# Block products with a fourth accumulator, down products of a stage's first tiles moved back, norm statistics later in PE's list

## The chip, the core and the metric

The kernel runs on one core of a Trainium2 chip. Its time is device time in microseconds (us) from the start of an execution to its end. Engines are named as in the profile: PE (TensorE: MATMUL, and PEld for its weight loads), DVE (VectorE), ACT (ScalarE), POOL (GpSimd) and SP (SyncE, which here only issues DMAs).

## What is computed

Two transformer-like blocks on 512 tokens of width 1024, all in fp32. Seven stages follow each other on the same residual x:

```python
h  = x + concat(gla(n), mla(n)) @ w_out          # n = rms_norm(x)            stage "mix"
h += square(relu(m @ w_up)) @ w_down             # 1024 -> 4096 -> 1024       stage "mlp"
h += (p @ w_proj) * sigmoid(n @ w_gate + b)      #                            stage "ple"
x += pool_mixer(rmsnorm(x))                      #                            stage "pool"
x += (silu(conv3(n @ w_gate)) * (n @ w_val)) @ w_out   # 1024 -> 2816 -> 1024 stage "ffn0"
x += chunk_attention(rmsnorm(x)) @ w_o           # 16 heads                   stage "att"
x += (silu(conv3(n @ w_gate)) * (n @ w_val)) @ w_out   #                      stage "ffn1"
```

Each stage begins with a norm over the 1024 channels: y = x * rsqrt(mean(x*x) + eps) * gain. The gain is applied to x on the way in; the factor rsqrt(...) of each token is applied to a product after it.

## The kernel before, in words

**Layout.** Activations lie transposed, channels on the 128 partitions and the 512 tokens along the free axis, as eight tiles `x[0..7]` of 128x512. Every operand of a product is split into a high and a low part (ACT rounds to the high part, DVE subtracts), and a product is three matmuls: high*high, high*low, low*high (`mm3`). So each 512 KB block of weights, a *unit*, is loaded into a tile `ws` (seven of them), split into `wh` and `wl` in two halves, and used by 24 matmuls. A splitter task runs two to three units ahead of PE.

**Block products.** The up products of mlp and the gate and value products of ffn0 and ffn1 are done four output tiles at a time (a *quad*). The 1024 input channels form two halves, the tokens two halves, and the four output tiles two pairs, which makes a 2x2 by 2x2 block product; it is done with seven block products and sums of blocks where the plain way has eight. The seven are the rows of `PHASES`: b11, b21, n3, n2, n1, b22, t4, each with the accumulator (PSUM bank) that it adds to, whether it is the first in that bank, and the weight tile that it reads. `quad_step` combines them: after b11 ACT copies bank 0 to `c1`, after b21 DVE adds bank 1 to it; n2, n1 and b22 go on adding in bank 0, and ACT copies the bank after n2 (`u2`) and after n1 (`u4`); n3 starts bank 2. DVE subtracts u4 from bank 2 (`c22`); t4 then adds to bank 2, and DVE subtracts u2 from it. `quad_row` multiplies each finished quarter by the norm's factors, and two quarters make a row that `finish` turns into activations. In the trace all of these banks are `pq`, and `u2`, `u4` are `u`.

**Weights of a quad.** `LOADS` gives the five loads of a quad and their place in the order of loads, counted in units from the quad's first. The tile `sum` is loaded three units early and has a second block added to it by a DMA that adds, on POOL's queue. It is split for n3; then a third block is added (`ADDED`) and it is split for n2; then a fourth, and it is split for b22. The tile `low` also has a block added on POOL's queue.

**First tiles and down units.** A stage's first four output tiles don't go by blocks: `first_tiles` fills four banks `pf` with plain products and waits for nothing but x, while DVE and ACT prepare the blocks of x for the quads (`prep_blocks`, `blocks_low`, `blocks_high`). The norm's statistics (`square`, `stats`) run beside it: squares are added over the eight tiles, PE sums over channels (`pst`), POOL takes the power -0.5, and PE spreads the factors of all tokens over the partitions (`psr`) to the row `R`. `first_out` multiplies the four banks by it. A *down unit* (`pdn`) multiplies finished activations by a block of the down weights into x. Quads are grouped (`QG1`: groups of one; `QG2`: 1, then four groups of 2, then 1 and 1), and down units of a group stand between the products of the next group's quads. `units_quads` writes that order out; `ORDERS` is the order of the seven products in a stage's first quad and in the others, and a tuple says behind which of them down units stand.

**Order of everything.** The program is written by generators that `drive` resumes at build time. `Pace` holds planned free times of each engine and ready times of each tile; a task is resumed when its tiles are planned ready at the time at which PE is planned free, the one with the lowest priority number first. Each engine's list is fixed by that. `sub` and `mul` go to DVE or POOL, whichever is planned to be done first; `help` is a planned extra cost of POOL, and with 1e3 POOL is never taken. It is 0.0 in mix and 1e3 from mlp on.

Of the kernel before, what the change touches and what calls it, by code (L numbers as in the profile page):

```python
# [35 lines left out]
def groups(n, most):  # L36
# [3 lines left out]
    for s in size:  # L40
# [8 lines left out]
QG2 = [1] + [2] * (FF2 // P // 4 - 1) + [1] * 2  # L49

PHASES = (("b11", 0, True, "a11"), ("b21", 1, True, "a12"), ("n3", 2, True, "sum"), ("n2", 0, False, "sum"),
          ("n1", 0, False, "low"), ("b22", 0, False, "sum"), ("t4", 2, False, "a22"))

ORDERS = (0, 1, 2, 3, 4, 6, 5), (2, 0, 1, 3, 4, 6, 5)

LOADS = (("sum", 0, -3, (2,)), ("a11", 0, 1, ()), ("a12", 1, 2, ()), ("low", 2, 1.5, (3,)), ("a22", 3, 5, ()))

ADDED = {2: 3, 3: 1}
GIVEN = {0: "a11", 1: "a12", 4: "low", 5: "sum", 6: "a22"}
# [124 lines left out]
class Block:  # L184
# [5 lines left out]
    PM, PG = 2, 3  # L190
    LAZY = 3, 2
    DEC, SCT = 1, 1
    HELP, TURN = (0.0, 1e3), 1.0

    def __init__(self, ctx, tc, a):
# [86 lines left out]
    def load_units(self, most=None):  # L282
        while (self.n_load < len(self.loads) and self.n_load - len(self.ws_freed) < self.most
               and (most is None or self.n_load < most)):
            _, n, src, cols, name, more = self.loads[self.n_load]
            t = self.sp.tile([P, 1024], F32, tag="ws", bufs=self.NL, name="ws")
            if self.n_load >= self.NL:
                self.pace.ready[t.tensor.name] = self.ws_freed[self.n_load - self.NL]
            self.nc.sync.dma_start(t[:, :cols], src)
            if name is None:  # L290
                self.loaded[n] = t
            else:
                n.tile[name] = t
                for block in more:
                    self.nc.gpsimd.dma_start(t, n.src[block], accum_op=OP.add)
            self.n_load += 1
# [187 lines left out]
    def square(self, norm, x, row=True, late=True):  # L484
        nc = self.nc
        sq = self.slot("sq")
        nc.scalar.activation(sq, x, AF.Square)
        if norm.acc is None:
            norm.acc = sq
        else:  # L490
            (nc.vector if late and norm.count > 5 else nc.gpsimd).tensor_add(norm.acc, norm.acc, sq)
        norm.count += 1
        if norm.count == KD:
            self.spawn(self.stats(norm, row), 1)

    def stats(self, norm, row):
        nc = self.nc
        yield self.room(7)
        yield [norm.acc]
        ps = self.bank("pst")  # L500
        for j in range(NT):
            nc.tensor.matmul(ps[:, j:j + 1], norm.acc[:, j * P:(j + 1) * P], self.ones[:, :1], start=True, stop=True,
                             skip_group_check=True)
        norm.acc = None
        norm.ms = self.small("ms", NT)
        nc.vector.tensor_scalar(norm.ms, ps[:, :NT], 1.0 / DM, EPS, op0=OP.mult, op1=OP.add)
        self.free()
        norm.r = self.power("r", norm.ms, NT)
        if not row:
            return  # L510
        yield [norm.r]
        dg = self.slot("dg")
        for j in range(NT):
            nc.vector.tensor_scalar(dg[:, j * P:(j + 1) * P], self.ident, norm.r[:, j:j + 1], None, op0=OP.mult)
        yield self.room(7)
        yield [dg]
        ps = self.bank("psr")
        nc.tensor.matmul(ps, self.ones, dg, start=True, stop=True)
        R = self.slot("R")
        nc.scalar.activation(R, ps, AF.Copy)  # L520
        self.free()
        norm.R = R
# [714 lines left out]
    @staticmethod  # L1237
    def units_quads(plain, src, downs, sizes):

        quads, units, order, wait = [Quad(src[4 * i:4 * i + 4]) for i in range(sum(sizes) - 1)], [], [], []  # L1240
        q, left = -1, sum(sizes)
        for g, n in enumerate(sizes):
            for i in range(n):
                left -= 1
                if q < 0:
                    order.append((q, 0))
                    units += plain
                else:
                    most = -(-len(wait) // (n - i)) if left else len(wait) - 2
                    for at, ph in enumerate(ORDERS[q > 0]):  # L1250
                        order.append((q, ph))
                        units.append(("quad", quads[q], ph))
                        for _ in range((4, 3, 6, 1)[:min(most, len(wait))].count(at)):
                            order.append(wait[0][:2])
                            units.append(wait.pop(0)[2])
                q += 1
            for w in wait:
                order.append(w[:2])
                units.append(w[2])
            wait = [("down", (g, u), x) for u, x in enumerate(downs[g])]  # L1260
        for w in wait:
            order.append(w[:2])
            units.append(w[2])
        return units, order
# [28 lines left out]
    def quads(self, norm, order, sizes, last, after, take, finish, late=None):  # L1293


        group = []
        for g, n in enumerate(sizes):
            group += [g] * n
        acts = [[None] * (n * last) for n in sizes]
        self.finish = finish  # L1300
        ps = quad = None
        for what, i in order:
            if what == "down":
                g, u = i
                yield from self.down(acts[g], u, after if g == len(sizes) - 1 else lambda m: None)
                continue
            if what < 0:
                yield from self.first_tiles(norm, take, acts[0])
                continue
            block, acc, first, _ = PHASES[i]  # L1310
            if quad is None:
                if late is not None and what == sum(sizes) - 2:
                    self.spawn(late(), 5)
                ps, quad = [None] * 3, {"norm": norm, "take": take, "rows": [None, None], "left": [2, 2],
                                        "acts": acts[group[what + 1]], "at": what + 1 - group.index(group[what + 1])}
            yield from self.unit(8, P)
            unit = self.got
            if first:
                yield self.room()
                ps[acc] = self.bank("pq%d" % acc)  # L1320
                self.pace.again.add(ps[acc].tensor.name)
            else:
                name = (None, None, None, "c1", "u2", "u4", "c22")[i]
                yield lambda: name in quad
                yield [quad[name]]
            b = norm.blocks[block]
            for k in range(4):
                yield lambda: b[k] is not None
                for w in range(2):
                    yield [*unit, *b[k]]  # L1330
                    self.mm3(ps[acc][:, w * 256:(w + 1) * 256], (unit[0][:, 4 * w + k], unit[1][:, 4 * w + k]), b[k],
                             first and k == 0 and w == 0, k == 3)
            self.used(ps[acc])
            if i != 2:
                self.spawn(self.quad_step(i, ps, quad), -3)
            if i == 5:
                ps = quad = None

    def quad_step(self, i, ps, quad):

        s, v = self.nc.scalar, self.nc.vector
        yield [ps[PHASES[i][1]]]
        if i in (0, 3, 4):
            name = {0: "c1", 3: "u2", 4: "u4"}[i]
            t = self.slot(name)
            s.activation(t, ps[0], AF.Copy)
            quad[name] = t
        if i == 1:
            yield lambda: "c1" in quad
            t = quad["c1"]  # L1350
            yield [t]
            v.tensor_add(t, ps[1], t)
            self.free()
            self.spawn(self.quad_row(quad, 0, 0, t), -2)
        elif i == 4:
            yield [t, ps[2]]
            v.tensor_sub(t, ps[2], t)
            quad["c22"] = t
            self.spawn(self.quad_row(quad, 1, 1, t), -2)
        elif i == 5:  # L1360
            yield from self.quad_row(quad, 0, 1, ps[0])
            self.free()
        elif i == 6:
            t = quad["u2"]
            yield [t, ps[2]]
            v.tensor_sub(t, ps[2], t)
            self.free()
            self.spawn(self.quad_row(quad, 1, 0, t), -2)

# [394 lines left out]
    def main(self, stages):  # L1764
# [13 lines left out]
        for i, st in enumerate(stages):  # L1778
# [8 lines left out]
            else:  # L1787
                nxt = None
                after = self.store
            yield from run[st](norm, after)  # L1790
            self.lazy, self.help, self.most = self.LAZY[1], self.HELP[1], self.NL
            norm = nxt


# [163 lines left out]
```

## Time and profile before

| | |
|---|---|
| time, median of 3 runs | 1721.99 us (1721.39 to 1725.96) |
| the profiled execution: time, span | 1723.74 us, 1722.0 us |
| mean granted clock of PE | 0.981 |
| busy: PE, DVE, ACT, POOL | 1645.4, 1256.3, 882.0, 265.5 us |
| DMA | 224.85 MB, 131 GB/s |

The span runs from the first instruction to the last. A busy PE has a matmul in it; its matmuls overlap. The granted clock is given as a share of 2.4 GHz, and in this trace it is 1.0 or 0.5. Stages by the trace: mix to 277 us, mlp to 628, ple and pool to 709, ffn0 to about 1084, att to about 1345, then ffn1.

### The profile page before, as it was taken

Reading aid. Unit: us, or ns where it says so; the run is one execution under the profiler, and the core shown is the slowest. Engines: PE = TensorE matmul, PEld = TensorE weight load, DVE = VectorE, ACT = ScalarE, POOL = GpSimd, SP = SyncE. Lnnn points to the kernel's source line nnn. Section 1 sums busy time; section 2 is a strip of 40 time slices with the busy share of each in tenths; the row PEclk is TensorE's granted clock in tenths of the full one; section 3 lists DMA queues with packets and bytes.
Section 4 is the critical chain, followed back from the end, with each engine's and each line's share of the span. In section 5 each row is a group of like instructions: output and inputs, shape, how many; then the busy total and the mean of one; then the engine's idle time right before and its main releaser. Section 6 shows DMA issues by size and latency. Waiting matters only on the chain. (4 is left out here: it accounts for less than half of the span.)

```text
span 1722.0 us, 27741 instructions
## 1 busy us (share of the span) xinstructions
PE 1645.4 (96%) x10640; PEld 1469.7 (85%) x10640; DVE 1256.3 (73%) x2436; ACT 882.0 (51%) x1711; POOL 265.5 (15%) x296
## 2 busy tenths in 40 slices
PE   7989899899999999989999998999999999999998
PEld 6878777799999978879999987989897789999896
DVE  7976769566666757978777767576679878777776
ACT  6635455444444545835454444466656655554542
POOL 3432212001000011211111100221210211111100
PEclk9999999899999999989999999999999999999999
DMA  7101222566666424267677654322223257776751
GB/s 271 50 26 37 85 76 80 133 167 160 161 162 165 150 86 126 62 153 194 177 194 198 174 147 123 111 74 75 74 86 86 86 141 203 186 202 175 180 139 49
DMA packets 66390, 224.85 MB, mean 131 GB/s; under 512 B 7617, under 2 KB 9554, under 8 KB 66258
## 3 DMA queue, kind: packets, MB, share of 16 engines
q1 hardware_dynamic: 50706, 166.46, 27.8%
q0 software_dynamic: 15552, 56.63, 18.9%
q8 instruction: 83, 1.36, 0.3%
q14 instruction: 49, 0.40, 0.1%
HBM read 220.96 MB, written 2.10 MB: 130 GB/s over the span
## 5 line engine op out<-in xcount | busy, mean ns | idle before, releaser
L147 ACT ACTIVATE wh<-ws 128x512 fp32r<-128x512 f32 x690 | 392.7, 621 | 289.7 <-PE pdn L147 140.6
L147 DVE TENSOR_TENSOR wl<-ws,wh 128x512 fp32r<-128x512 f32 x682 | 451.1, 703 | 87.3 <-ACT wh L147 87.0
L147 PE MATMUL pq<-xsh,wh 128*128 128x256 f32 x864 | 246.8, 286 | 4.3 <-ACT u L147 4.3
L147 PE MATMUL pq<-xsl,wh 128*128 128x256 f32 x864 | 245.2, 284 | 0.0
L147 PE MATMUL pq<-xsh,wl 128*128 128x256 f32 x864 | 245.1, 284 | 0.0
L147 DVE TENSOR_TENSOR x<-x,pdn 128x512 f32<-128x512 f32 x177 | 119.8, 682 | 122.6 <-PE pdn L147 122.6
L147 PEld LDWEIGHTS pq<-xsh,wh 128*128 128x128 f32 x864 | 166.3, 192 | 7.4 <-ACT u L147 5.5
L147 PEld LDWEIGHTS pq<-xsl,wh 128*128 128x128 f32 x864 | 166.4, 193 | 1.9 <-issue 0.7
L147 POOL DMA_DIRECT2D ws<-in_w_f x80 | 70.4, 895 | 631.7 <-DVE wl L147 381.1
L147 PEld LDWEIGHTS pq<-xsh,wl 128*128 128x128 f32 x864 | 166.4, 193 | 0.0
L147 PE MATMUL pdn<-yh,wh 128*128 128x512 f32 x352 | 140.2, 398 | 6.4 <-ACT yh L147 6.4
L147 PE MATMUL pdn<-yl,wh 128*128 128x512 f32 x352 | 140.0, 398 | 3.5 <-DVE yl L147 3.4
L147 PE MATMUL pdn<-yh,wl 128*128 128x512 f32 x352 | 138.4, 393 | 0.0
L147 PE MATMUL pq<-xch,wh 128*128 128x256 f32 x432 | 123.1, 285 | 1.9 <-ACT wh L147 1.9
L147 PE MATMUL pq<-xch,wl 128*128 128x256 f32 x432 | 123.3, 286 | 1.2 <-DVE wl L147 1.2
L147 PE MATMUL pq<-xcl,wh 128*128 128x256 f32 x432 | 122.9, 284 | 0.0
L147 PE MATMUL paq<-wh,xsh 128*128 128x256 f32 x384 | 111.4, 290 | 1.8 <-DVE akk L147 1.8
L147 PE MATMUL paq<-wh,xsl 128*128 128x256 f32 x384 | 108.6, 283 | 0.0
L147 PE MATMUL paq<-wl,xsh 128*128 128x256 f32 x384 | 108.6, 283 | 0.0
L147 PE MATMUL pdn<-hh,wh 128*128 128x512 f32 x256 | 101.3, 396 | 4.7 <-ACT hh L147 4.7
L147 PE MATMUL pdn<-hl,wh 128*128 128x512 f32 x256 | 101.5, 397 | 0.9 <-DVE hl L147 0.8
L147 PE MATMUL pdn<-hh,wl 128*128 128x512 f32 x256 | 100.6, 393 | 0.0
(329 smaller groups left out, 3902.7 us busy)
## 6 DMA issues: line engine op xcount, KB each, us to landing
ws<-in_w_f SPq DMA_DIRECT2D x108, 512.0 KB, 4.0
ws<-in_w_f POOLq DMA_DIRECT2D x80, 512.0 KB, 5.5
ws<-in_w_fo SPq DMA_DIRECT2D x44, 512.0 KB, 4.2
ws<-in_w_up SPq DMA_DIRECT2D x39, 512.0 KB, 3.4
ws<-in_w_down SPq DMA_DIRECT2D x32, 512.0 KB, 3.3
ws<-in_w_up POOLq DMA_DIRECT2D x28, 512.0 KB, 5.5
ws<-in_w_out SPq DMA_DIRECT2D x8, 512.0 KB, 3.4
ws<-in_w_gate SPq DMA_DIRECT2D x8, 512.0 KB, 3.2
```

The source lines that it names most:

```text
L147: return call(*args, **kw)
```

## The change

- t4 gets a bank of its own (accumulator 3, the first in it), and stands ahead of n1. After n2 DVE subtracts u2 from bank 2 at once (a new instruction in each quad), after n1 it subtracts u4 from bank 2, which is then free, and after t4 it adds bank 3. PE no longer waits for c22.
- The loads of `low` and `a22` change places in the order of loads.
- Down units stand behind other products: none in the first quad after the first tiles, and later in the others.
- `stats` gets priority -4 instead of 1, and for all norms but the first the sum of squares and the tile for `psr` are planned ready 2.0 us later.
- `help` is set by stage: 1e3 in mlp, ffn0 and ffn1, and 0.0 in mix, ple, pool and att.
- The planned ready time of a load's tile is that of the load `most` places earlier (three in mix, seven later) instead of seven.

```diff
 PHASES = (("b11", 0, True, "a11"), ("b21", 1, True, "a12"), ("n3", 2, True, "sum"), ("n2", 0, False, "sum"),
-          ("n1", 0, False, "low"), ("b22", 0, False, "sum"), ("t4", 2, False, "a22"))
-ORDERS = (0, 1, 2, 3, 4, 6, 5), (2, 0, 1, 3, 4, 6, 5)
-LOADS = (("sum", 0, -3, (2,)), ("a11", 0, 1, ()), ("a12", 1, 2, ()), ("low", 2, 1.5, (3,)), ("a22", 3, 5, ()))
+          ("n1", 0, False, "low"), ("b22", 0, False, "sum"), ("t4", 3, True, "a22"))
+ORDERS = (0, 1, 2, 3, 6, 4, 5), (2, 0, 1, 3, 6, 4, 5)
+LOADS = (("sum", 0, -3, (2,)), ("a11", 0, 1, ()), ("a12", 1, 2, ()), ("low", 2, 2.5, (3,)), ("a22", 3, 4, ()))
...
+    LATE = 2.0
...
-            if self.n_load >= self.NL:
-                self.pace.ready[t.tensor.name] = self.ws_freed[self.n_load - self.NL]
+            if self.n_load >= self.most:
+                self.pace.ready[t.tensor.name] = self.ws_freed[self.n_load - self.most]
...
-            self.spawn(self.stats(norm, row), 1)
+            self.spawn(self.stats(norm, row), -4)
...
     def stats(self, norm, row):
         nc = self.nc
+        late = 0.0 if norm.gain == self.GAIN["mix"] else self.LATE
+        self.pace.ready[norm.acc.tensor.name] += late
...
+        self.pace.ready[dg.tensor.name] += late
         yield self.room(7)
         yield [dg]
...
-                    most = -(-len(wait) // (n - i)) if left else len(wait) - 2
+                    most = 0 if q == 0 else -(-len(wait) // (n - i)) if left else len(wait) - 2
...
-                        for _ in range((4, 3, 6, 1)[:min(most, len(wait))].count(at)):
+                        for _ in range(((5, 2, 6, 3) if i else (5, 6, 4, 3))[:min(most, len(wait))].count(at)):
...
-                ps, quad = [None] * 3, {"norm": norm, ...
+                ps, quad = [None] * 4, {"norm": norm, ...
...
-                name = (None, None, None, "c1", "u2", "u4", "c22")[i]
+                name = (None, None, None, "c1", "u2", "u4")[i]
                 yield lambda: name in quad
-                yield [quad[name]]
...
-        if i == 1:
+        if i == 3:
+            yield [t, ps[2]]
+            v.tensor_sub(t, ps[2], t)
+        elif i == 1:
...
         elif i == 4:
             yield [t, ps[2]]
             v.tensor_sub(t, ps[2], t)
-            quad["c22"] = t
+            self.free()
...
         elif i == 6:
             t = quad["u2"]
-            yield [t, ps[2]]
-            v.tensor_sub(t, ps[2], t)
+            yield [t, ps[3]]
+            v.tensor_add(t, ps[3], t)
...
+            self.help = self.HELP[st in self.QUADS]
             yield from run[st](norm, after)
-            self.lazy, self.help, self.most = self.LAZY[1], self.HELP[1], self.NL
+            self.lazy, self.most = self.LAZY[1], self.NL
```

## Rows read from the trace of the kernel before

**Rows 1.** The page's first part: busy us (share of the span) xinstructions

```profile
PE 1645.4 (96%) x10640; PEld 1469.7 (85%) x10640; DVE 1256.3 (73%) x2436; ACT 882.0 (51%) x1711; POOL 265.5 (15%) x296
```

**Rows 2.** Busy by windows: stretch, its length, busy of each engine, PEclk, DMA share, GB/s

```profile
861.00:904.05 43.05, 43.05 (x318) 41.13 (x317) 34.20 (x59) 22.91 (x41) 5.25 (x6) 1.00 0.75 194
...
284.00:324.00 40.00, 32.82 (x151) 25.59 (x150) 29.58 (x61) 20.57 (x42) 6.77 (x6) 0.87 0.48 111
726.00:770.00 44.00, 35.74 (x194) 29.81 (x193) 33.26 (x64) 19.13 (x35) 7.96 (x7) 0.88 0.56 144
1362.00:1400.00 38.00, 32.77 (x177) 28.13 (x175) 29.24 (x58) 18.84 (x37) 6.54 (x5) 0.87 0.55 139
```

**Rows 3.** Waits of PE: who waited for whom, us in total, times, longest

```profile
PE pst L147 <- DVE sq L147: 7.8, 5, 2.4
```

**Rows 4.** Timeline of PE, ffn1's last quad: start, us, instruction, [idle before, releaser]

```profile
1681.61 0.38 PE L147 MATMUL pq<-xsh,wh 128*128 128x256 f32 x1 [0.69 <-ACT u L147]
...
1687.88 0.80 PE L147 MATMUL pq<-xt,wh 128*128 128x256 f32 x2 [3.13 <-DVE u L147]
...
1692.10 0.28 PE L147 MATMUL pq<-xsh,wh 128*128 128x256 f32 x1
```

**Rows 5.** Timeline of PE, the first group of one quad, ffn0 and ffn1

```profile
993.01 0.40 PE L147 MATMUL pdn<-yh,wh 128*128 128x512 f32 x1
...
1003.10 0.28 PE L147 MATMUL pq<-xsh,wh 128*128 128x256 f32 x1
...
1629.62 0.40 PE L147 MATMUL pdn<-yh,wh 128*128 128x512 f32 x1
...
1638.47 0.28 PE L147 MATMUL pq<-xsh,wh 128*128 128x256 f32 x1
```

**Rows 6.** Timeline of PE, mlp's first quad: down unit, two products, down unit

```profile
308.32 0.49 PE L147 MATMUL pdn<-hh,wh 128*128 128x512 f32 x1
...
323.66 0.28 PE L147 MATMUL pq<-xch,wh 128*128 128x256 f32 x1
...
329.41 0.40 PE L147 MATMUL pdn<-hh,wh 128*128 128x512 f32 x1
...
334.88 0.28 PE L147 MATMUL pq<-xsh,wh 128*128 128x256 f32 x1
```

**Rows 7.** Timeline of PE, first quads: ffn0 n1 and t4; ffn1 n2, n1, t4

```profile
753.80 0.38 PE L147 MATMUL pq<-xsh,wh 128*128 128x256 f32 x1 [0.75 <-ACT u L147]
...
768.46 0.40 PE L147 MATMUL pq<-xt,wh 128*128 128x256 f32 x2
...
1388.43 0.39 PE L147 MATMUL pq<-xch,wh 128*128 128x256 f32 x1 [0.56 <-ACT wh L147]
...
1395.25 0.38 PE L147 MATMUL pq<-xsh,wh 128*128 128x256 f32 x1 [0.75 <-ACT u L147]
...
1405.00 0.40 PE L147 MATMUL pq<-xt,wh 128*128 128x256 f32 x2
```

**Rows 8.** Timeline of POOL and ACT, ffn0's first quad

```profile
739.32 1.84 POOL L147 DMA_DIRECT2D ws<-in_w_f  x2 [3.35 <-DVE xsl L147]
...
748.52 3.76 ACT L147 ACTIVATE wh<-ws 128x512 fp32r<-128x512 f32 x7 [0.78 <-DMA ws<-in_w_f]
```

**Rows 9.** Timeline of POOL and DVE, pool stage

```profile
714.67 1.29 POOL L147 TENSOR_TENSOR sq<-sq 128x512 f32<-128x512 f32 x1 [0.45 <-ACT sq L147]
...
713.61 2.90 DVE L147 TENSOR_TENSOR wl<-ws,wh 128x512 fp32r<-128x512 f32 x2
```

**Rows 10.** Groups of DVE over the span: busy us, mean ns of one | idle before

```profile
L147 DVE TENSOR_TENSOR wl<-ws,wh 128x512 fp32r<-128x512 f32 x682 | 451.1, 703 | 87.3 <-ACT wh L147 87.0 <-issue 0.2
...
L147 DVE TENSOR_TENSOR u<-pq,u 128x512 f32<-128x512 f32 x54 | 37.3, 691 | 60.7 <-ACT u L147 33.8 <-PE pq L147 26.9
```

**Rows 11.** Tile wl: on POOL (ns min/median/max, first and last start); on DVE in att

```profile
L147 POOL TENSOR_TENSOR wl<-ws,wh x8: 1265/1289/1358, 34.4 to 243.4; 128x512 fp32r<-128x512 f32 x8
...
1075.00:1345.00 270.00, 41.83 (x65) 1.00 0.26 84
```

More of the change, by code (lines that the diff above doesn't have):

```diff
@@ L1313, in quads @@
                     self.spawn(late(), 5)
-                ps, quad = [None] * 3, {"norm": norm, "take": take, "rows": [None, None], "left": [2, 2],
+                ps, quad = [None] * 4, {"norm": norm, "take": take, "rows": [None, None], "left": [2, 2],
                                         "acts": acts[group[what + 1]], "at": what + 1 - group.index(group[what + 1])}
```

## The prediction

> **What bounds the kernel now.** I read the page's first part, then the busy time by windows, the PE waits, and the PE timeline at each place where the windows show a gap. The page has PE busy 1645.4 us of a span of 1722.0 [rows 1]: no other engine comes near, so only two things can be won, the 76.6 us in which PE idles and the time at half clock. The windows say where they are not: in the middle of a stage PE is busy 43.05 of 43.05 us at clock 1.00 with DVE at 34.2 [rows 2]. They are at the beginnings of the three stages of block products. In 284 to 324 (mlp) PE idles 7.2 us and the mean clock is 0.87; in 726 to 770 (ffn0) 8.3 us and 0.88; in 1362 to 1400 (ffn1) 5.2 us and 0.87 [rows 2]. I price the clock as window times its deficit (0.5 is 1.2 GHz, 1.0 is 2.4): 5.2, 5.3 and 4.9 us, so 12.4, 13.5 and 10.2 us lie over each beginning. Idle and price of the clock overlap a little; I leave that to the range.
>
> **Unit prices.** A block product lasts 2.87 us (n3 and n2 fill 323.66 to 329.41) and a down unit 5.47 (329.41 to 334.88) where nothing waits [rows 6].
>
> **Step 1: fourth accumulator, t4 ahead of n1.** Today t4 accumulates onto n3's bank, so PE must wait until n1 is done, ScalarE has copied it and VectorE has subtracted it. In the middle of a stage down units lie between, and hide it. The last quad of ffn1 has none: n1 begins at 1681.61 after a wait of 0.69 for the copy, t4 at 1687.88 after 3.13, b22 at 1692.10 [rows 4]. That is 6.27 + 4.22 us for two products worth 5.74, so 4.75 lost (the wait, and t4 at half clock). After the change n2, t4, n1 and b22 follow each other; the wait of 0.7 moves from ahead of n1 to ahead of b22, the rest has no cause left. ffn0's last quad has the same order; I count it alike: 9.5 us for both. mlp's last quad keeps two down units and gives nothing.
> What it adds: a third subtraction a quad, 27 in all at 0.69 us [rows 10], 18.7 us of DVE. In mid stage DVE has 8.9 us free in 43 [rows 2] and a quad with its downs is shorter than that window, so the cover is ample: 0 there. At a beginning it costs what is counted in step 3. It also adds a PSUM bank: three are held by a quad instead of two while down units ask for room, and t4 of a stage's first quad must wait until the first tiles leave one of their four; with three products ahead of it (8.6 us) I cost that at 0, bounds 0 and 3 a stage.
>
> **Step 2: later places for down units.** Where ffn's groups go from two quads to one, the first down unit stands behind only two products and reads activations of the quad just ended: 993.01 to 1003.10 and 1629.62 to 1638.47 [rows 5], 10.09 and 8.85 us for 5.47, so 8.0 lost. In the new order four products stand ahead of it, 5.7 us more, which is over the 4.6 and 3.4 it was late. 8.0 won. In the other quads the downs only move behind work that is there anyway: 0.
>
> **Step 3: the three beginnings.** The first quad loses its down units to the end of its group (mlp) or to the next quad (ffn). mlp's first lasts from 308.32 to 323.66, 9.9 us too long [rows 6]. In ffn0, n1 and the down unit take 753.80 to 768.46, 14.66 for 8.34; in ffn1 1395.25 to 1405.00, 9.75 [rows 7]: 6.3 and 1.4 lost. The statistics add their share: PE waited 7.8 us in five places for the sum of squares, 2.4 at most [rows 3]; the 2 us of LATE cover nearly all.
> What is late next is n2. Its tile is n3's tile with one more block added by a DMA on POOL's queue, issued only when n3's split has been read. In ffn0 POOL issues it at 739.32, and ScalarE's split, waiting for that DMA, begins at 748.52 [rows 8]: 9.2 us. If PE reaches n2 sooner, it waits there. In ffn1 the same product lasts 6.82 us, 1388.43 to 1395.25 [rows 7]. In mlp the two down units that hid this DMA are gone. The loads of low (later) and a22 (sooner) move with it on SP's queue and, for low's own addition, on POOL's, so that less stands ahead of n2's addition; a gain of 0 to 3 us in each stage, of which I take 1.
> The second limit is DVE. It was busy 29.6, 33.3 and 29.2 us in these windows [rows 2] and does not get less (0.7 more each). So at most 9.7, 10.0 and 8.1 us can go there, 27.8 together; the low end is 0, or 3 us lost if n2's wait brings the half clock with it. The downs of mlp are the surest, so I take 8, 6.5 and 5: 19.5 us. The new wait of n1's copy ahead of b22 costs 0.7 in each first quad: 2.1.
> Two of the five waits for the statistics lie in ple and the attention stage, outside the windows; at the mean of 1.6 [rows 3] they are 3.1, of which I take 2.5. The inverse root and the row of factors come up to 4 us later; in ple eight products, in the others the first quad lie between, so 0, bounds 0 and 2 a norm.
>
> **Step 4: POOL helps again.** The last lines of the diff are not in its title: with `help` at 0.0 in ple, pool and att the planner may give a split's subtraction to POOL when DVE is behind. POOL did 8 in mix at 1.29 us [rows 11]; DVE takes 0.70 [rows 10], and att alone has 65 of them [rows 11]. The two engines disturb each other: with POOL's addition running from 714.67, DVE's pair of 713.61 took 2.90 us instead of 1.41 [rows 9, 10]; it lost 1.5, and I put that at 0.8 for each of its two. So a move saves DVE 0.7, costs it up to 0.8 and delivers 0.6 later. Bounds: 5 us won (seven moves where DVE is short and nothing is held up) to 91 lost (all of att's 65 at 1.4). At mix's 8 I expect about eight in att and six in ple and pool, 14 in all, most of them under PE's work; I take 3 lost.
> The Trainium skill, page "SBUF — State Buffer", section "Who interferes with whom", says that a VectorE instruction with two SBUF inputs contends with a GpSimd instruction that reads SBUF, and that the one behind is fully blocked. By that, 14 moves cost DVE 14 x (1.29 - 0.70) = 8 us, an estimate with the durations of this trace; by the row it is 14 x (0.8 - 0.7), about 1. The trace agrees in kind, with 0.8 of 1.3.
>
> **The sum.** 9.5 + 8.0 + 19.5 + 2.5 + 3 x 1 for the loads = 42.5 won; 2.1 + 3 lost; another 4.5 taken off because the whole list of work is planned anew, and the stretches that have no wait now can get one (bounds 2 won, 10 lost). 33 us won. The profiled execution took 1723.74 (span 1722.0 and 1.74 around it), 1.75 over the median of the runs. 1723.74 - 33 = **1691 us**.
>
> **Rivals.**
> - *n2 and DVE keep the beginnings* (0.26). The products get to n2 sooner and wait there for the addition. For it: the 9.2 us of [rows 8], and DVE busy to three quarters in windows that are full of PE waits. Against it: the 9.9 us of mlp's down unit were a wait for activations, not for weights. Then 9.5 + 8.0 + 2.5 stay, and of the beginnings a net 1 after the other losses: 21, **1703 us**.
> - *Nothing moves* (0.08). On top of the first rival the fourth bank delays t4 by its 3 us in each of three beginnings (9), and the late row of factors costs its 2 in five norms (10). 21 - 19 = 2 us: **1722 us**. For it: eight banks, four of them under first tiles. Against it: the row's factors are needed only after three products.
> - *POOL's help slows it* (0.08). One mechanism, in att, ple and pool: POOL's subtraction holds up DVE's, and splits come late to a PE that is nearly full. For it: the pair of [rows 9]. Against it: only 8 operations went to POOL in all of mix [rows 11]. It decides when the loss passes the rest of the gain, 36 us: some 26 moves at 0.6 + 0.8 with no cover. With 32 moves it is 45 lost against 36: **1733 us**. The page of the Trainium skill named under step 4 describes that hold.
> - The forecast, 1680 to 1700, has 0.58.
>
> **Range and chances.** 1676 to 1712: the low end has the beginnings at their DVE limit (8 more) and no loss from planning or POOL (7.5 more), the high end takes in the first rival with 8 us lost to POOL. The last two rivals stay out, 0.16, with 0.04 below. 0.3% is 5.2 us, about what measurements of this kernel can tell apart. Faster: 0.58 + 0.26 = 0.84; same 0.08; slower 0.08.
>
> **What will show it.** The PE wait "pq <- DVE u" goes, and t4 in the last quads lasts 2.9 us; the group u<-pq,u counts 81. Down units last 5.5 us at both switches. PE's pst waits fall below 2 us in all. In the beginnings: a wait of n2 ("pq <- ACT wh") of 1 to 4 us each if I am right, 5 or more with half clock if the first rival is. DVE's busy time is near 1275. POOL's count of wl, 8 now, says how much step 4 did; above 35, with new idle PE time between 1075 and 1345, I am wrong on it. A total of PE idle and half clock not reduced by a third would show the whole forecast wrong.

## The result, and the profile after

The changed kernel takes **1682.09 us**, median of 4 runs (1680.26 to 1685.6), against 1723.97 (1721.39 to 1726.4) of the kernel before in the same comparison: ratio 0.976, 95% interval 0.9734 to 0.9785. 41.9 us are won; 33 were predicted (1691), in a range of 1676 to 1712. The number lies in the range, but the sum behind it was right in two terms only. Other terms were some 9 us too high, and gains of some 20 us were not in it; that these partly cancel is luck.

The profiled execution took 1680.26 us (span 1678.5, mean clock 0.992). First part of its page, beside [rows 1]:

```profile
PE 1626.3 (97%) x10640; PEld 1459.2 (87%) x10640; DVE 1262.8 (75%) x2444; ACT 882.0 (53%) x1714; POOL 282.4 (17%) x312
```

PE idles 52.2 us where it idled 76.6, 24.4 less. The other 19 us are clock: 1722 us at a deficit of 0.019 is 32.7, 1678.5 at 0.008 is 13.4. So both reserves that the prediction named were drawn on.

The same windows as in [rows 2], moved along so that they lie at the same distance from the stage's first tile (length, busy of PE, PEld, DVE, ACT, POOL, PEclk, DMA share, GB/s; the first is in the middle of ffn0):

```profile
841.96:885.01 43.05, 43.05 (x301) 40.41 (x301) 35.89 (x63) 23.77 (x42) 4.34 (x5) 1.00 0.71 194
271.69:311.69 40.00, 36.23 (x230) 32.13 (x229) 33.96 (x68) 25.74 (x51) 5.02 (x6) 1.00 0.56 145
706.96:750.96 44.00, 37.28 (x239) 34.35 (x239) 33.84 (x68) 20.61 (x38) 5.55 (x6) 0.88 0.59 154
1325.55:1363.55 38.00, 31.19 (x197) 28.01 (x195) 28.48 (x57) 18.64 (x36) 5.13 (x7) 0.96 0.50 131
```

Only mlp's beginning is mended (3.8 us of idle at full clock, where idle and clock had cost 12.4). ffn0's still loses 6.7 idle and 5.3 of clock, ffn1's 6.8 and 1.5. A window of fixed length holds more of the stage's work than before (239 matmuls for 194 in ffn0's), so these figures say where time is still lost, not what was won.

PE's waits (us in total, times, longest), beside [rows 3]:

```profile
PE pq L147 <- ACT u L147: 10.1, 8, 2.1
PE pl L147 <- ACT wh L147: 7.8, 1, 7.8
PE pq L147 <- ACT wh L147: 5.3, 3, 3.3
PE pdn L147 <- DVE yl L147: 3.0, 4, 1.8
PE psr L147 <- DVE dg L147: 2.2, 1, 2.2
```

The waits for the squares (7.8 us) and for DVE's u (t4 in the last quads, [rows 4]) are gone. Largest are now waits for the copy u by ACT: 10.1 us in eight, where before they were 4.3 us in six. (The wait of pl is at the start of the kernel, 8.6 us before.) DVE's groups, beside [rows 10], and POOL's share of the splits, beside [rows 11]:

```profile
L147 DVE TENSOR_TENSOR wl<-ws,wh 128x512 fp32r<-128x512 f32 x665 | 437.0, 699 | 91.0 <-ACT wh L147 90.8
...
L147 DVE TENSOR_TENSOR u<-pq,u 128x512 f32<-128x512 f32 x81 | 55.6, 688 | 45.3 <-ACT u L147 35.2 <-PE pq L147 10.1
```

```profile
L147 POOL TENSOR_TENSOR wl<-ws,wh 128x512 fp32r<-128x512 f32 x25 | 33.3, 1347 | 114.0 <-ACT wh L147 85.0 <-issue 28.9
```

81 subtractions of u, as counted. Of the 25 splits on POOL, by the counts of a_help (4) and a_helpatt (21) below, 4 lie in mix, 17 in att and 4 in ple and pool: 21 by the help, where 14 were expected. DVE's busy time is 1262.8 us where 1275 was forecast, since those splits left it. Idle time and price of the clock fell from 109.3 to 65.6 us, by more than the third that the prediction had named as its sign.

**By stage**, from PE's timeline (a stage of block products begins with its first `pf` matmul, ple with `ppj`, att with `paq`; ffn1 is counted to PE's last matmul, 4.0 us ahead of the span's end). By this, att ends at 1349.7 us in the kernel before. The kernels of the experiments below stand in the same table:

| us | mix | mlp | ple, pool | ffn0 | att | ffn1 |
|---|---|---|---|---|---|---|
| before | 276.95 | 351.23 | 80.72 | 374.94 | 265.86 | 368.27 |
| **after** | 264.69 | 344.26 | 80.91 | 364.83 | 258.56 | 361.22 |
| b_load | 264.30 | 353.11 | 80.70 | 375.16 | 265.78 | 368.21 |
| b_help | 274.61 | 352.42 | 84.33 | 376.00 | 260.29 | 373.56 |
| b_statslate | 274.65 | 349.00 | 79.49 | 380.63 | 264.02 | 373.23 |
| a_only_quads | 273.88 | 348.89 | 77.82 | 371.13 | 265.08 | 366.77 |
| a_help | 264.31 | 344.21 | 80.42 | 364.78 | 264.04 | 361.53 |
| a_helpatt | 267.80 | 346.42 | 80.42 | 364.42 | 258.58 | 361.68 |
| a_olddowns | 265.77 | 354.52 | 81.16 | 381.65 | 258.58 | 378.33 |
| a_t4first | 264.16 | 347.37 | 80.78 | 368.09 | 258.60 | 369.14 |
| a_lowlate | 266.60 | 346.05 | 80.90 | 368.44 | 258.57 | 363.88 |
| a_lowlate_t4 | 266.93 | 347.26 | 80.63 | 366.26 | 258.55 | 361.34 |
| a_low15 | 264.69 | 349.59 | 85.50 | 361.39 | 258.58 | 361.03 |
| a_pool0 | 264.99 | 344.37 | 79.50 | 364.92 | 258.58 | 360.99 |

One row is one execution. Between executions with the same list of PE, mix varied by up to 3.6 us, mlp by up to 2.2 and att by less than 1. The three stages that the prediction spoke of gave 24.1 us of the 43.5. **mix gave 12.3 and att 7.3**, where it had expected nothing and a loss.

### The profile page after: what moved, and what is told of

It is laid out like the page before. It is cut to its first block, busy times and chain, and to the rows that moved or that the text cites. A ratio compares the mean times of both kernels' runs of the same rounds, so it can differ in the third digit from the quotient of the medians.

```text
span 1678.5 us, 27783 instructions
## 1 busy us (share of the span) xinstructions
PE 1626.3 (97%) x10640; PEld 1459.2 (87%) x10640; DVE 1262.8 (75%) x2444; ACT 882.0 (53%) x1714; POOL 282.4 (17%) x312
## 3 DMA queue, kind: packets, MB, share of 16 engines
q1 hardware_dynamic: 50706, 166.46, 28.1%
## 5 line engine op out<-in xcount | busy, mean ns | idle before, releaser
L147 DVE TENSOR_TENSOR wl<-ws,wh 128x512 fp32r<-128x512 f32 x665 | 437.0, 699 | 91.0 <-ACT wh L147 90.8
L147 PE MATMUL pq<-xsh,wh 128*128 128x256 f32 x864 | 246.6, 285 | 10.1 <-ACT u L147 10.1
L147 PEld LDWEIGHTS pq<-xsh,wh 128*128 128x128 f32 x864 | 167.1, 193 | 12.9 <-ACT u L147 11.7
```

Of the source, the lines that this page charges most:

```text
L147: return call(*args, **kw)
```

## Experiments

The first four each put one part of the change into the kernel before.

**b_load**: the planner's due times of loads alone.

```diff
-            if self.n_load >= self.NL:
-                self.pace.ready[t.tensor.name] = self.ws_freed[self.n_load - self.NL]
+            if self.n_load >= self.most:
+                self.pace.ready[t.tensor.name] = self.ws_freed[self.n_load - self.most]
```

> The kernel before with one edit of the change alone: the planner's due time of a load goes by the number of loads in flight (3 in the mix stage, 7 later), not by the 7 buffers. Theory: the profiles show mix 12.3 us shorter after the change, and this edit is the only one that orders PE's list anew in mix, so the whole of it comes here: 1711 to 1713 us, all of the difference ahead of the first tile of mlp. Rival: mix is shorter because the statistics of the norms stand elsewhere or because POOL helps, and the order of the loads is worth nothing: 1722 to 1726 us.

Measured: 1715.92 us, ratio 0.994 (0.9918 to 0.9962): 8 to 10 us. mix is 12.65 shorter than in the profile of before, about 10 shorter than in the three others that leave mix alone. mlp is 1.9 longer, but its list of PE is that of before, so this is no effect of the edit. Theory held as to the place; the time lies between its 1711 to 1713 and the rival's 1722. Two stretches of mix in the kernel before, then in this one (columns as above), and PE's waits of mix in each:

```profile
80.00:100.00 20.00, 16.17 (x105) 13.52 (x103) 16.04 (x46) 10.18 (x22) 9.42 (x19) 0.83 0.10 40
180.00:200.00 20.00, 16.27 (x107) 13.39 (x106) 15.22 (x49) 5.79 (x14) 3.27 (x4) 0.83 0.00 0
```

```profile
80.00:100.00 20.00, 19.27 (x146) 16.46 (x144) 18.39 (x56) 8.93 (x23) 6.93 (x10) 1.00 0.08 27
180.00:200.00 20.00, 18.23 (x144) 15.06 (x145) 17.10 (x56) 6.97 (x16) 6.54 (x11) 1.00 0.32 103
```

```profile
PE mt L147 <- DVE prob L147: 6.1, 6, 2.0
PE po L147 <- DVE sct L147: 5.6, 4, 1.9
```

```profile
PE mt L147 <- DVE prob L147: 1.9, 2, 1.6
...
PE po L147 <- DVE sct L147: 1.0, 1, 1.0
```

Before, PE stood idle 3.8 us in each stretch and the clock fell. The two groups of waits, 11.7 us, shrink to 2.9. With due times that fit the three loads in flight, the planner puts other matmuls (x146 for x105 in the first stretch) into these gaps.

**b_help**: POOL's help in ple, pool and att alone.

```diff
+            self.help = self.HELP[st in self.QUADS]
             yield from run[st](norm, after)
-            self.lazy, self.help, self.most = self.LAZY[1], self.HELP[1], self.NL
+            self.lazy, self.most = self.LAZY[1], self.NL
```

> The kernel before with one edit alone: POOL may take a weight split's subtraction in ple, pool and the attention stage. Theory: the attention stage's 7.3 us come from here, ple and pool get nothing: 1716 to 1718 us, POOL's count of such subtractions 8 + 14 to 18. Rival one (my prediction): the help costs about 3 us: 1725 to 1728. Rival two: attention is shorter because its statistics come later: 1722 to 1726 here, with its stage as long as before, 266 us.

Measured: 1729.64 us, ratio 1.0027 (1.0011 to 1.0043), by the ratio slower by 4.6 us (2 to 7). Theory and my prediction were each half right: att is 5.6 shorter, but ple and pool 3.6 longer and ffn1 5.3. The trace shows where: in the pool stage PE has one new wait, 2.9 us for ACT's xsh, and in ffn1's first quad it waits 2.4 us for wh, 2.3 for yh and 1.0 for yl, where before it waited 0.6, 0.5 and 0.2. What made these late is not shown.

**b_statslate**: statistics later alone (priority -4, and 2 us on `norm.acc` and `dg`).

```diff
-            self.spawn(self.stats(norm, row), 1)
+            self.spawn(self.stats(norm, row), -4)
...
+        self.pace.ready[norm.acc.tensor.name] += late
...
+        self.pace.ready[dg.tensor.name] += late
```

> The kernel before with one edit alone: the statistics of a norm 2 us later in PE's list. Prediction: PE's waits for the sum of squares fall from 7.8 us to under 2 us; 2.5 us of them in ple and attention, the rest at the beginnings of the block product stages: 1717 to 1720 us. Rival: PE only waits for the next thing instead (weights, activations), since the work of VectorE and ScalarE ahead of it is the same: 1722 to 1725 us with the same idle time of PE.

Measured: 1726.79 us, ratio 1.0008 (0.9993 to 1.0023): nothing won. The prediction fell; the rival's 1722 to 1725 was near. ple, pool and att are 3.1 shorter, mlp 2.2, but ffn0 5.7 and ffn1 5.0 longer. In ffn0 the row of factors (psr) comes 32.7 us behind the stage's first tile, 28.1 before. PE reaches the first quad's down unit 0.8 us sooner, and its activations come 3.2 later; this kernel:

```profile
756.65 0.80 PE L147 MATMUL pdn<-yh,wh 128*128 128x512 f32 x1 [6.24 <-ACT yh L147]
757.38 0.80 PE L147 MATMUL pdn<-yl,wh 128*128 128x512 f32 x1
```

6.24 us of wait, and then matmuls of 0.8 us where 0.4 is normal, at a granted clock of 0.50 (756.65 to 762.00).

**a_only_quads**: the edits of `PHASES`, `ORDERS`, `LOADS`, `units_quads`, `quads` and `quad_step` alone.

```diff
+ORDERS = (0, 1, 2, 3, 6, 4, 5), (2, 0, 1, 3, 6, 4, 5)
...
+                    most = 0 if q == 0 else -(-len(wait) // (n - i)) if left else len(wait) - 2
```

> The kernel before with the edits of the block products alone: the fourth accumulator, the new order of the seven products, the moved loads and the later places of the down products; statistics, loads' due times and POOL's help as before. Theory (the parts add up by stages): mlp, ffn0 and ffn1 give 24 us together less what the later statistics give, mix, ple, pool and attention nothing: 1700 to 1705 us. Rival one: the later statistics are needed for it, and without them the beginnings keep their stalls: 1708 to 1712. Rival two: the parts do not add up, replanning decides: under 1695 or over 1715.

Measured: 1707.53 us, ratio 0.9898 (0.9874 to 0.9922). 17.6 us, but only 7.6 in the three stages (2.3, 3.8, 1.5), not 24: the parts don't add up by stages, and the total lies just short of rival one's numbers. What is left, in the first quad of ffn0:

```profile
734.45 2.05 PE L147 MATMUL psr<-dg,ones 128*128 128x512 f32 x2 [4.34 <-DVE dg L147]
```

PE waits 4.3 us for the row of factors. The row itself is late: DVE had what the inverse root needs at 727.5, but in POOL's list low's own addition stands ahead of the root and waits 15.5 us for low's load:

```profile
731.46 0.88 POOL L147 DMA_DIRECT2D ws<-in_w_f  x1 [15.53 <-DMA ws<-in_w_f]
732.07 1.33 POOL L147 TENSOR_TENSOR r<-ms,mhalf 128x4 f32<-128x4 f32 x1
```

That wait is not what the total lacks, though. In ffn0 and ffn1 the first quad ends as soon as in a_help below, which has the later statistics (56.7 us behind the stage's first tile for 57.4, and 55.1 for 54.6). The difference, 6.4 and 5.2 us, lies in the first down unit of the third quad: 11.91 and 12.24 us here, 6.05 in both stages there. In ffn0 it stands between these two rows, and its longest wait is 1.75 us, for yl:

```profile
806.58 0.40 PE L147 MATMUL pdn<-yh,wh 128*128 128x512 f32 x1
...
818.50 0.28 PE L147 MATMUL pq<-xsh,wh 128*128 128x256 f32 x1
```

So the two parts need each other: the later statistics win nothing on the kernel before, and some 15 us on this one (a_help). Why the operands of that down unit come late without them is open. The four ratios multiplied give 0.987; the change has 0.976.

The next kernels take one part out of the changed kernel or alter it.

**a_help**: POOL's help undone (the diff of b_help, reversed).

> The changed kernel with POOL's help in ple, pool and attention undone. So far the help alone, on the kernel before, cost 4.6 us: attention 5.6 shorter, ple and pool 3.6 longer, ffn1 5.3 longer. Theory one (it costs the same within the change): attention 5.6 longer, ple and pool 3 shorter, ffn1 4 to 5 shorter than after the change: 1677 to 1681 us. Theory two (the later order at ffn1's beginning takes its loss away and keeps its gain): attention 5 to 7 longer, ffn1 the same, ple and pool 3 shorter: 1684 to 1687 us.

Measured: 1686.58 us, ratio 0.9768 (0.9741 to 0.9795). Theory two, but for ple and pool, which it had 3 us shorter: att is 5.5 longer, all other stages are within 0.5 us, ffn1 too. Within the change the help wins 5.5 us in att and costs nothing that shows. The totals, with intervals that overlap, don't show it by themselves; the stage does, which took 258.55 to 258.60 us in all eight kernels that have the change's list there. PE's waits in att, here and in the changed kernel:

```profile
PE ao L147 <- ACT probT L147: 4.8, 5, 1.4
PE paq L147 <- DVE akk L147: 1.8, 3, 0.6
```

```profile
PE at L147 <- DVE prob L147: 2.0, 3, 1.4
PE paq L147 <- DVE akk L147: 1.2, 2, 0.6
```

The five waits for probT go when POOL takes splits. Set beside a_only_quads, which differs from a_help by the late statistics and by mix's due times (which alone moved none of these stages beyond what executions differ, b_load), the late statistics give mlp 4.7, ffn0 6.4, ffn1 5.2 and att 1.0, and cost ple and pool 2.6.

**a_helpatt**: the help in mix and att only.

```diff
-            self.help = self.HELP[st in self.QUADS]
+            self.help = self.HELP[st not in ("mix", "att")]
```

> The changed kernel with POOL's help in the attention stage alone, not in ple and pool. Theory: ple and pool lose their 3 us (81 to 78, as in the kernel with the block products' edits alone), ffn0 does not change, attention keeps its 258.6: 1678 to 1680 us. Rival: the 3 us are not POOL's, but come from the later statistics: 1681 to 1684.

Measured: 1684.34 us, ratio 0.9747 (0.9719 to 0.9775). ple and pool stay at 80.4: rival held as to the stage: the 3 us there are not POOL's.

**a_olddowns**: the old places of the down units in the new order.

```diff
-                    most = 0 if q == 0 else -(-len(wait) // (n - i)) if left else len(wait) - 2
+                    most = -(-len(wait) // (n - i)) if left else len(wait) - 2
...
-                        for _ in range(((5, 2, 6, 3) if i else (5, 6, 4, 3))[:min(most, len(wait))].count(at)):
+                        for _ in range((4, 3, 6, 1)[:min(most, len(wait))].count(at)):
```

> The changed kernel with the old places of the down units: in the first quads, and in the switches from two quads to one behind two products. Prediction: the two switches lose 8 us again (first down unit there 10.1 and 8.9 us instead of 5.5), and the three first quads get their down units back, with waits for the activations, 12 to 20 us: 1702 to 1710 us. Rival: with the fourth accumulator the first quads' time is set by DVE and ScalarE, with the downs in it or not, and only the switches lose: 1688 to 1692 us.

Measured: 1728.1 us, ratio 1.0007 (0.999 to 1.0024). 46 us worse than the change, more than either forecast: without the new places the change gives nothing in all. mix and att keep their 18 us, and mlp, ffn0 and ffn1 lose 20 against the kernel before. PE's waits, and ffn0's first down unit, of this kernel:

```profile
PE pdn L147 <- ACT yh L147: 22.8, 8, 9.8
PE pq L147 <- ACT u L147: 18.5, 27, 0.7
```

```profile
751.83 0.80 PE L147 MATMUL pdn<-yh,wh 128*128 128x512 f32 x1 [9.79 <-ACT yh L147]
```

The first line is the expected part: first quads and switches. The second is one I had not thought of: in the new order b22 stands behind n1 in every quad, and must wait 0.7 us for its copy unless a down unit lies between, in all 27 quads. The place "5" in the new tuple is that cover. In my working the wait was counted in the three first quads alone.

**a_t4first**: t4 ahead of n2 in first quads, a22 loaded one place earlier.

```diff
-ORDERS = (0, 1, 2, 3, 6, 4, 5), (2, 0, 1, 3, 6, 4, 5)
+ORDERS = (0, 1, 2, 6, 3, 4, 5), (2, 0, 1, 3, 6, 4, 5)
...
```

> The changed kernel with t4 ahead of n2 in the first quad of mlp, ffn0 and ffn1, and a22's load one place earlier. Theory: n2 waits 0.5, 1.4 and 3.3 us for the weights that the addition on POOL's queue completes, and runs at half clock after it; with t4's 2.9 us ahead the wait goes in mlp and ffn0 and falls under 1 us in ffn1. Against it n1 then stands right behind n2 and waits 0.7 to 1 us for its copy: 3 to 6 us won in all, 1676 to 1679 us. Rival: DVE and ScalarE prepare the blocks and weights of the whole first quad late, so each product that comes sooner waits by as much (t4's activations are the last that are prepared): 1681 to 1684 us, with the same end of the first quad.

Measured: 1695.07 us, ratio 0.9821 (0.9794 to 0.9848), 13 us worse than the change; both fell. n2's wait did fall (3.5 to 2.6 us in ffn1, none in the others), but n1 waits 4.6 to 6.1 us for the copy of n2. ACT's timeline in ffn1 of this kernel shows why:

```profile
1356.75 2.19 ACT L147 ACTIVATE wh<-ws 128x512 fp32r<-128x512 f32 x4 [5.04 <-DMA ws<-in_w_f]
...
1364.72 2.19 ACT L147 ACTIVATE wh<-ws 128x512 fp32r<-128x512 f32 x4 [5.07 <-DMA ws<-in_w_f]
1366.82 0.57 ACT L147 ACTIVATE u<-pq 128x512 f32<-128x512 f32 x1
```

The copy u stands behind a split of weights that waits 5 us for the addition by DMA. ACT takes its list in order, so a late DMA holds a copy that has all it needs. The changed kernel has the same in small; in ffn1 n1 waits 1.10 us for this copy:

```profile
1356.68 1.15 ACT L147 ACTIVATE wh<-ws 128x512 fp32r<-128x512 f32 x2 [4.16 <-DMA ws<-in_w_f]
1357.74 0.58 ACT L147 ACTIVATE u<-pq 128x512 f32<-128x512 f32 x1
```

**a_lowlate**: low's own addition issued at the split of n2's weights.

```diff
...
+        if ph in (3, 4) and "low" in quad.tile and not quad.summed:
+            nc.gpsimd.dma_start(quad.tile["low"], quad.src[3], accum_op=OP.add)
+            quad.summed = True
```

> The changed kernel with one thing moved: low's own addition on POOL's queue is issued at the split of n2's weights, not at low's load. In the changed kernel it stands first in POOL's queue at each of the three beginnings and waits 15 to 16 us there for low's load; the inverse root of the norm (POOL) and n2's addition stand behind it. Theory (POOL's queue holds the beginnings): the root comes 6 us sooner, PE's wait for dg (2.2 us in ffn0) goes, n2's waits of 1.1, 1.7 and 3.5 us go or fall under 1, and the half clock after them with it: 1670 to 1677 us. Rival (the beginnings are bound by DVE's and ScalarE's work, the queue only looks late): n2 waits less and n1 or b22 by as much more, 1680 to 1684 us. Rival two: low's addition now lands too late for n1, slower than after the change: 1685 to 1692.

Measured: 1689.15 us, ratio 0.979 (0.977 to 0.9811), 7 us more than the change by the medians, though the intervals overlap. ffn0 and ffn1 are 3.6 and 2.7 longer. That is in the second rival's range, but not by its mechanism (n1 waits for no weights). The theory's first step was there: n2's waits fall from 1.67 and 3.51 to 0.98 and 1.00 in ffn0 and ffn1, and the second quad begins 7 us sooner in both. But then PE stands before the first down unit, 6.70 and 6.53 us; ffn1 in this kernel:

```profile
1383.66 0.80 PE L147 MATMUL pdn<-yh,wh 128*128 128x512 f32 x1 [6.53 <-ACT yh L147]
1384.39 0.80 PE L147 MATMUL pdn<-yl,wh 128*128 128x512 f32 x1
```

The operand yh was held by ACT's list, as the copy u was in a_t4first. DVE's last step ahead of it (qr) ends at 1377.12, but a split that waits for an addition stands before it:

```profile
1376.43 0.69 DVE L147 TENSOR_TENSOR qr<-qr,fb 128x512 f32<-128x512 f32 x1
```

```profile
1379.67 2.19 ACT L147 ACTIVATE wh<-ws 128x512 fp32r<-128x512 f32 x4 [4.26 <-DMA ws<-in_w_f]
...
1382.99 0.61 ACT L147 ACTIVATE yh<-qr 128x512 fp32r<-128x512 f32 x1
```

ffn0 has the same, with a wait of 4.44 us. In the changed kernel this yh is done 55.4 us behind the stage's first tile, and PE comes to its unit at 63.5. So the first tiles' activations were not late by themselves: in a_lowlate the input of yh was there when PE came (1377.13). The moved addition brings n2 forward and makes a later split late. One wait of 6.53 us, and a unit behind it that lasts 10.4 us for 5.47 (granted clock 0.50 to 1391 us), cost more than the 7 us won before it.

**a_lowlate_t4**: both of the last two.

> The same with t4 ahead of n2 in the first quads as well. In the changed kernel that order cost 13 us, since n1 then waited 4.6 to 6.1 us for the copy of n2's product, which stood in ScalarE's queue behind splits that waited for additions. Theory: with POOL's queue free those splits are no longer late, and n2 has 2.9 us more time: the wait for the copy falls to about 0.7 to 1 us, 1668 to 1675 us. Rival: the split of b22's weights waits for the addition that follows n2's split whatever stands before, and the copy stays behind it: 1683 to 1690 us, slower than the kernel with the moved addition alone.

Measured: 1686.98 us, ratio 0.9776 (0.9755 to 0.9798): in the rival's range, but not slower than a_lowlate, as it had said. Its mechanism is there: n1 waits 3.3 to 5.5 us for the copy of n2 in all three first quads. The two edits together don't help either.

**a_low15**: low and a22 loaded at the old places.

```diff
-... ("low", 2, 2.5, (3,)), ("a22", 3, 4, ()))
+... ("low", 2, 1.5, (3,)), ("a22", 3, 5, ()))
```

> The changed kernel with the loads of low and a22 back at their old places (low one place earlier, a22 one later). Prediction: the moved loads are worth 0 to 3 us a stage, about 1: 1683 to 1686 us here. Rival (low's addition stands ahead of n2's on POOL's queue with either place, and an earlier load lets it pass sooner): n2's waits at the beginnings fall: 1676 to 1680 us.

Measured: 1685.1 us, ratio 0.9766 (0.9745 to 0.9786): 3.0 us by the medians, as predicted, though the two intervals overlap. It is not 1 us a stage: mlp loses 5.3 (ACT's split ahead of the copy waits 4.60 for its DMA there, and n1 4.96 for the copy), ple and pool 4.6 (PE waits 2.8 us for ACT's xsh there, as in b_help), and ffn0 wins 3.4.

**a_pool0**: no late statistics in the pool stage, the one place where they cost. The list of PE differs in this alone.

```diff
-        late = 0.0 if norm.gain == self.GAIN["mix"] else self.LATE
+        late = 0.0 if norm.gain in (self.GAIN["mix"], self.GAIN["pool"]) else self.LATE
```

> The changed kernel with the 2 us of delay for the statistics taken away in the pool stage alone; in PE's list the sum of squares there moves 24 matmuls (2.9 us) forward, and nothing else does. In the changed kernel it stands after the last pu product, with nothing behind it that PE could do while POOL and VectorE finish the factors: it takes 2.84 us to the next matmul instead of 0.8 to 0.9, and pp then waits 1.90 us for u. Theory: both go, ple and pool fall from 80.9 to 78 us, the rest is as after the change: 1678 to 1680.5 us, 2 to 3 under the changed kernel. Rival: the sum of squares is not ready 2.9 us sooner (VectorE's last additions), PE waits ahead of it instead and the stage stays at 80 to 81 us: 1681 to 1684 us.

Measured: 1680.45 us, ratio 0.975 (0.9726 to 0.9774). ple and pool 79.5 instead of 80.9, half of what was expected; both sides were half right. PE there, changed kernel, then this one:

```profile
677.43 0.95 PE L147 MATMUL pst<-ones,sq 128*128 128x1 f32 x8
680.27 2.07 PE L147 MATMUL pp<-pm,u 128*128 128x144 f32 x8 [1.90 <-DVE u L147]
```

```profile
675.92 1.05 PE L147 MATMUL pst<-ones,sq 128*128 128x1 f32 x8 [1.51 <-DVE sq L147]
...
681.28 1.97 PE L147 MATMUL pp<-pm,u 128*128 128x144 f32 x15
```

pp no longer waits, but the sum of squares now does, 1.51 us. The kernel has the lowest median of all, but its interval overlaps the change's: no gain over it is shown.

## Why the prediction came out as it did

The terms, with "lost" as the length of PE's blocks over 2.88 us a product, 5.47 a down unit and 5.44 a first tile's unit, summed over the place:

| term | predicted | lost before -> after | won |
|---|---|---|---|
| two last quads | 9.5 | 5.8 -> 0.9, 5.6 -> 0.9 | 9.5 |
| two switches | 8.0 | 4.6 -> 0, 3.4 -> 0 | 8.0 |
| three beginnings, new waits and loads in them | 19.5 - 2.1 + 3 | 13.7 -> 6.7, 18.8 -> 14.6, 14.7 -> 12.8 | 13.1 |
| statistics in ple, pool, att | 2.5 | att 1.8; ple and pool gained about nothing | 2 |
| POOL's help | -3 | att 264.04 -> 258.56 (a_help, after) | 5.5 |
| replanning, the rest of the three stages | -4.5 | ends 3.4 -> 6.4, middles 3.4 more | -6 |
| mix's due times | not in the sum | b_load | 10 to 12 |

**Right.** Step 1 and step 2, to a tenth of a microsecond in all: t4 in the last quads takes 2.88 us, with the wait of 0.7 moved to b22 as forecast, and the down units at the switches take 5.47. ffn1 after the change, last quad (t4, n1, b22) and switch:

```profile
1641.13 0.40 PE L147 MATMUL pq<-xt,wh 128*128 128x256 f32 x2
...
1644.01 0.28 PE L147 MATMUL pq<-xsh,wh 128*128 128x256 f32 x1
...
1647.73 0.38 PE L147 MATMUL pq<-xsh,wh 128*128 128x256 f32 x1 [0.69 <-ACT u L147]
```

```profile
1599.13 0.40 PE L147 MATMUL pdn<-yh,wh 128*128 128x512 f32 x1
...
1604.59 0.40 PE L147 MATMUL pq<-xt,wh 128*128 128x256 f32 x2
```

Both were read as a wait at one place with its cover counted out. The n2 waits of 1.1, 1.7 and 3.5 us lie in the 1 to 4 that I had named.

**Too large: step 3.** The sentence that fell short is "What is late next is n2". Late next were also the copies by ACT: six waits of 0.7 to 2.1 us, 8.7 together, for the 2.1 that I took. n1's stand behind splits that wait 1.7 to 4.2 us for a DMA, and b22's 2.1 us in ffn0 and ffn1 behind the work that piled up on ACT after such a split. Where n2 came sooner (a_t4first, a_lowlate), the same list held the copy, or the first activation. The bound by DVE, 27.8, was no near one: ACT waiting in order for DMAs came first. mlp, where four covered down units follow, won 7.0 of the net 8.3 that I gave it, ffn0 4.2 of 6.8, ffn1 1.9 of 5.3.

**Wrong in sign: step 4.** I priced a moved split by what it does to DVE (0.7 saved, up to 0.8 lost) and took the cover for granted. In att the chain runs over ACT's probT, and 17 moved splits took five waits of it away. On the kernel before, the same edit does cost 4.6 us, by its effect on the stages beside att; the trace shows the waits there, not what makes them. The pair in [rows 9] was misread a little: the first of its two subtractions lost 0.46 us to an earlier addition on POOL, the second 1.1 to the one named, not 0.8 each to one.

**Not seen: the load's due time.** I put it under "replanning, 4.5 lost", by its size in the diff. With 10 to 12 us it is the second largest part. The view of PE's waits could have shown where: beside the row in [rows 3] it had "mt <- DVE prob" and "po <- DVE sct", 11.7 us in mix, and I looked at the stages that the title names. Gains put some 9 us too high (step 3, the ends) and gains of some 20 left out (mix 11, help 8.5) made the forecast 9 us too long. The forecast was closer than its parts deserved.

**Open:** why ffn1 and ple are longer with the help alone and not within the change, why the third quad's down unit is late without the later statistics, and what a list of ACT would give in which copies and activations stand ahead of splits that wait for additions: no kernel tried it. A longer delay of the statistics was not tried either.

## What to carry to other kernels

Where a planner writes the instruction lists, a wrong due time costs as much as a wrong order: look at each edit of the planner by the waits of the stage that it plans, not by its size. Look for what holds the engine that PE waits for: here ACT, whose list put splits that wait for a DMA ahead of copies and activations whose inputs were ready. Taking away one wait of PE then only moved it, and one stand of 6.5 us, with half clock behind it, cost more than the 7 us won. And parts of a change are priced together: here four parts with ratios of 0.99, 1.00, 1.00 and 0.99 make 0.976.

## What the hardware showed that was not expected

POOL's inverse root of 128x4 takes 1.34 us in ffn1 of the changed kernel, with DVE idle, and 3.36 us in a_lowlate, where DVE does subtractions of two operands beside it. (The kernel before has it too: 2.94 us beside such subtractions in mlp, ffn0 and ffn1, 1.03 to 1.04 in ple, pool and att.) So in a_lowlate the root of ffn1 begins 3.6 us sooner behind the stage's first tile and ends only 1.6 sooner:

```profile
1341.42 1.34 POOL L147 TENSOR_TENSOR r<-ms,mhalf 128x4 f32<-128x4 f32 x1
```

```profile
1345.10 3.36 POOL L147 TENSOR_TENSOR r<-ms,mhalf 128x4 f32<-128x4 f32 x1 [11.77 <-DVE ms L147]
```

```profile
1344.93 1.29 DVE L147 TENSOR_TENSOR wl<-ws,wh 128x512 fp32r<-128x512 f32 x2
1346.13 1.43 DVE L147 TENSOR_TENSOR xsl<-xn,xsh 128x256 fp32r<-128x256 f32 x4
```

DVE's instructions take no longer than elsewhere: here POOL alone pays, 2.0 us, where in [rows 9] DVE paid. By the Trainium skill, page "SBUF — State Buffer", section "Who interferes with whom", the one that comes behind is blocked while the other holds the port; this trace agrees in kind, with 2.0 us lost beside some 2.5 us of DVE's work. One place does not fit: in att of the changed kernel the root at 1066.00 takes 1.04 us, the two subtractions that begin 0.03 us behind it take 0.71 and 0.68, and so neither lost anything.
